# Four row tiles of the first three units multiplied into six open PSUM banks before the last four feature tiles are modulated

## The chip, the cores and the metric

The kernel runs on one core of one Trainium2 chip. The metric is device time in microseconds (us) of one launch; lower is better. A core has engines that run beside each other, each through its own list of instructions in order: TensorE (PE, matrix products into PSUM), VectorE (DVE), ScalarE (ACT), GpSimd (POOL) and SyncE (SP, which here only issues the transfers of weights). They wait for each other by semaphores. An engine whose next instruction waits does nothing else, and everything behind that instruction waits with it.

## The reference

A backbone of two layers on 512 tokens (256 of context, 256 latent) with 1024 features, all in float32. Each layer mixes tokens in three branches, and then has a feed-forward part. What this case touches is the very beginning of the first layer:

```python
mod_l = (jax.nn.silu(c) @ w_mod[l] + b_mod[l])[:, None, :]
sh1, sc1, g1, sh2, sc2, g2 = jnp.split(mod_l, 6, axis=-1)
# mixer_sublayer(x * (1.0 + sc1) + sh1, ..., w_in[l], ...), the context tokens with a modulation of their own:
(hq_l, hff_l, hfb_l, hi_l, hg_l, aq_l, ak_l, av_l, mz_l, mx_l, mdt_l, gt_l) = jnp.split(h_lat @ w_in, IN_SPLITS, axis=-1)
# branch C, mamba_inputs(mx_l, mdt_l, ...) and then ssd_scan:
u = jax.nn.silu(dwconv_centred(xbc, conv_w) + conv_b)
xs, bm, cm = jnp.split(u, [MB_INNER, MB_INNER + MB_BC_WIDTH], axis=-1)
dt = jax.nn.softplus(dt_raw.reshape(n, t, 2, MB_HEADS).astype(F32) + dt_bias.astype(F32))
```

Before the first product of `w_in` can run, the modulation's matrix must have been read as far as shift and scale go (2048 columns by 1024 rows of float32, 8 MB), and the tokens must have been scaled and shifted by it.

## The kernel before

**Products.** Every float32 operand is split into two float32r parts whose sum it is: `hh` and `hl` of the activations (eight row tiles of 128 features by 512 tokens), `wh` and `wl` of the weights. A product is then three matmuls, hi·hi, hi·lo, lo·hi (`mm3`, L347). A unit is 256 columns of a weight matrix: two output tiles of 128 columns, each in a PSUM bank of its own, summed over eight row tiles. That is 2 × 8 × 3 = 48 matmuls of 128x512 (`unit_f`, L360). PSUM has three banks for units (`pg`), four for all that is smaller (`ps`), and one more.

**Weights.** The class `Weights` streams all blocks through SBUF in one planned order. A block is 512 KB: four row tiles by 256 columns, so a unit has two, its first half (row tiles 0 to 3) and its second (4 to 7). SP issues a block's transfer (L115) into one of four buffers `wraw` (L150). When PE's program comes to a block, four further blocks have been asked for and two more split (L157): ACT copies the upper part `wh` (L125), DVE subtracts and leaves `wl` (L126); there are three buffers of each. A transfer into a buffer waits until the block that lay there four blocks earlier has been read, and SP's transfers go out in their order, so one that waits holds all behind it.

**Modulation.** 512 columns of the modulation come from four blocks of 256 rows (`mod_step`, L276). These blocks are not split: PE reads them from `wraw` itself, with 8 small matmuls a block, each recorded twice by the profile. After the fourth, DVE copies, transposes and adds the bias (L287 to L289). Columns j=0 and j=1 are the shift of feature tiles 0 to 3 and 4 to 7; j=2 and j=3 the scale of them. The modulation that is needed later comes as one block after every unit (`tick`).

**The start.** `run` (L1426) computes the modulation of j=0 and 2, loads feature tiles 0 to 3 of the tokens (on ACT's queue), and modulates and splits them (`modulate_first`, L322: two `h` instructions, `hh` on ACT, `hl` on DVE for a tile); the same for j=1 and 3 and feature tiles 4 to 7. `plan` (L1386) has the 16 blocks of this in the order j = 0, 2, 1, 3. `layer` (L1441) then calls `ssd_dt` (L619: a product of 64 columns, then a long chain of small DVE and ACT instructions `dx`, `dm`, `dy`, `dr`, `dz`, `dp`, at whose end PE transposes the result, `dtT`) and `ssd_in` (L714: units mx 0, mx 1 and bc of the first group; six tiles `craw` leave PSUM, each goes through a convolution of one ACT and four DVE instructions, L701). Then `Weave` (L72) lays the next group's units beside the first group's scan, which takes the convolved tokens (`xtok`), dt and, by a round trip to DRAM, the decays.

**Order.** A scheduler with a cost model of its own fixes each engine's order when the program is built; on the chip that order isn't changed.

Of the kernel before, what the change touches and what calls it, by code (L numbers as in the profile page):

```python
# [13 lines left out]
P = 128  # L14
DM = 1024
ND = 8
# [4 lines left out]
T = SEQ + CTX  # L21
ALPHA = (2 * DEPTH) ** 0.25
FFN = 2816
# [10 lines left out]
# columns of the per-channel parameters of a layer  # L34
# [19 lines left out]
def stagger(a, b, n):  # L54
    """a, and from its step n on b beside it"""
    for _ in range(n):
        next(a, None)
        yield
    live = [a, b]
    while live:  # L60
        for g in list(live):
            if next(g, g) is g:
                live.remove(g)
            else:
                yield
# [6 lines left out]
class Weave:  # L72
    """Two strands of work: the steps of the side strand are spread over those of the main one and stay a
    little behind it, so that the main strand's next products never queue behind the end of a side chain."""
# [4 lines left out]
    def __call__(self, main, side, nm, ns, lead=0, lag=0):  # L79
        """nm and ns: the steps of each, lag: the part of the side strand, in steps of main, left for the next call"""  # L80
# [11 lines left out]
class Weights:  # L92
    """Streams weight blocks [128, k, c] through SBUF: each block is loaded once
    and split into two float32r parts whose sum is the float32 value."""
# [49 lines left out]
class Net:  # L144
    def __init__(self, tc, io, ctx):
# [13 lines left out]
        self.weave = Weave()  # L159
        self.ticks, self.tick_plan, self.tick_run = [], 0, 0  # L160

# [4 lines left out]
    def x(self, name="x"):  # L166
        """like a, for tiles that would otherwise queue behind the other strand's"""
        return self.wp.tile([P, 512], F32, tag="x", name=name, bufs=self.n_x)
# [45 lines left out]
    def rsqrt(self, x, n):  # L214
        """x <- x ** -1/2 on a few columns: a first guess from the exponent and three Newton steps"""
# [46 lines left out]
    def lower_bounds(self):  # L262
        """the second layer's: the softmax over two layers as a sigmoid"""
# [7 lines left out]
    def mod_spec(self, l, j, c):  # L271
        """512 columns from 512 j, rows [256 c, 256 c + 256)"""
# [27 lines left out]
    def tick(self):  # L300
        """a piece of the modulations that are needed later"""
# [10 lines left out]
    def load_x(self, d0, d1):  # L312
        """feature-major tokens, [context | latent]"""
# [8 lines left out]
    def modulate_first(self, d0, d1):  # L322
        """h = x (1 + sc) + sh"""
# [23 lines left out]
    def mm3(self, out, xh, xl, yh, yl, first, last):  # L347
        """out += (xh + xl)^T (yh + yl)"""
# [4 lines left out]
    def plan_w(self, key, w, cols, kt=ND):  # L353
        """a unit: 256 columns of a weight matrix, in blocks of four row tiles"""
# [5 lines left out]
    def unit_f(self, key, rng, x=None, kt=ND):  # L360
        """feature-major: two tiles of 128 columns by the tokens rng[m]"""
        xh, xl = x or (self.hh, self.hl)
        out = [self.pg() for _ in rng]
        for h in range(0, kt, 4):
# [5 lines left out]
        self.tick()  # L370
        return out

    def unit_raw(self, key, ln):
        """two tiles of 128 columns before the layer norm's statistics are there: products with the rows times
        the gains, and with the gains and biases as two more tokens"""
# [20 lines left out]
    def raw_end(self, ln, e, j):  # L396
        """the statistics put in: a tile but for the bias, and the bias"""
# [7 lines left out]
    def raw_split(self, ln):  # L405
        """the next rows times the gains as split operands, with the gains and biases behind them"""
# [17 lines left out]
    def unit_t(self, key, js):  # L424
        """token-major: pairs js of token tiles by 256 columns"""
# [23 lines left out]
    def hgrn_in(self, l, p, wc, st):  # L449
        """projections of a pair of heads and everything that reads them from PSUM"""  # L450
# [38 lines left out]
    def hgrn_head(self, l, st, m, wc, oh, ol):  # L489
        """One head: attention over all pairs of tokens by levels of halving. At level h a block of 2h tokens  # L490
        is halved; the forward direction reads keys of the first half from queries of the second, the
        backward direction the other way. K = [forward | backward] keys times the decay to the end
        (start) of their half, Q = [backward | forward] queries times the decay over their half."""
# [10 lines left out]
        def total(h):  # L504
            """products of the decays over blocks of h, [forward | backward] of T / h each"""
# [5 lines left out]
        def grow(h):  # L511
            """to halves of 2h"""
# [106 lines left out]
    def ssd_dt(self, l):  # L619
        """step sizes, their logarithms and the decays' running sums, (stream, direction, head) on partitions"""  # L620
# [60 lines left out]

    def ssd_plan_x(self, l, g):
        w = self.io["w_in"][l]
        if g == 0 and l == 0:
            self.ssd_dt_plan(l)
        for i in range(2):
# [14 lines left out]
    def conv(self, l, r, n, t0):  # L701
        """depthwise conv over time, feature-major"""
# [11 lines left out]
    def ssd_in(self, l, g, wc, st, early=None):  # L714
# [13 lines left out]
        else:  # L728
            for i in range(2):
                ps = self.unit_f(("mx", l, g, i), [(0, T)] * 2)  # L730
                st["x"] += [self.conv(l, self.evac(ps[m], 0), 4 * g + 2 * i + m, 0) for m in range(2)]
                yield
            ps = self.unit_f(("bc", l, g), [(0, T), (q0, T)])
# [6 lines left out]
    def silus(self, tiles):  # L740
        """together, after the exponentials before them: one switch of the activation table"""
# [15 lines left out]
    def ssd_scan(self, l, g, st, dts, wc, ys):  # L757
        """both directions' scans of a group: within each stream by its decay matrix, from the context by its end states"""
# [85 lines left out]
    def ssd_out(self, l, g, ys, zs, wc, om):  # L844
        """gate and grouped RMS norm"""
# [23 lines left out]
    def quarters(self, tiles, n):  # L869
        """sum over partitions of every fourth tile, on 32 partitions each"""  # L870
# [9 lines left out]
    def colmean(self, tiles, n):  # L880
        """mean over partitions and tiles, on every partition"""
# [691 lines left out]
```

## Time and profile before

| | |
|---|---|
| three runs | 2701.3 to 2703.74 us, median 2702.61 |
| profiled execution: span | 2706.7 us |
| PE busy | 2619.4 us, 97% of the span |
| DVE busy | 1782.5 us, 66% |
| ACT busy | 1232.1 us, 46% |
| first two slices of 20 us: PE busy | 8.65 and 13.46 us |
| first two slices of 20 us: DMA engines' busy share | 0.91 and 0.98 |

For the profiled execution there is no time beside its span. It is 4.1 us over the median. PE is the busiest engine by far, yet in the first 40 us it has work for 22 us only, and the DMA engines are full: there the weights of the modulation arrive.

### The profile page before, as it was taken

The page shows a single profiled execution, that of the slowest core. Times are in us where ns is not written, and L with a number is a line of the kernel's source. Part 1 is how long each engine was busy: PE and PEld are TensorE (multiplying, and loading weights), DVE is VectorE, ACT ScalarE, POOL GpSimd, SP SyncE. Part 2 cuts the span into 40 slices and gives each one's busy share as a digit, 9 for nine tenths or more (in the row PEclk, how much of TensorE's full clock was granted, in tenths as well). Part 3 has the DMA queues.
Part 4 walks back from the last instruction along what each step waited for, and adds up shares of the span by engine and source line. Part 5 has one row for each costly group of instructions (what it writes and reads, how often), then busy time and mean ns, then how long its engine had stood idle before and what let it go on. Part 6 is the DMA issues. An engine that isn't in the chain of part 4 may idle for free.

```text
span 2706.7 us, 46300 instructions
## 1 busy us (share of the span) xinstructions
PE 2619.4 (97%) x18660; PEld 2148.0 (79%) x18660; DVE 1782.5 (66%) x3708; ACT 1232.1 (46%) x2030; POOL 192.4 (7%) x320
## 2 busy tenths in 40 slices
PE   7999999999999999999999999899999999999999
PEld 5767767788888897777888877677878898878998
DVE  5887776756555675456433367887867778867555
ACT  3555554532333324535432236566554344465543
POOL 0111010000000001100000000111110011111000
PEclk9999999999999999999999999899999999999999
DMA  6566555543444445352333323555763353445553
GB/s 238 152 179 176 150 164 149 155 123 114 122 135 130 128 125 172 105 175 63 101 94 101 94 78 90 140 164 154 212 183 108 97 144 109 144 131 181 169 182 102
DMA packets 298951, 374.41 MB, mean 138 GB/s; under 512 B 16432, under 2 KB 251984, under 8 KB 298736
## 3 DMA queue, kind: packets, MB, share of 16 engines
q1 hardware_dynamic: 271568, 284.21, 34.9%
q0 software_dynamic: 25728, 84.61, 11.0%
q8 instruction: 147, 2.41, 0.4%
q10 hardware_dynamic: 1440, 2.62, 0.3%
q14 instruction: 68, 0.56, 0.1%
HBM read 355.27 MB, written 16.12 MB: 137 GB/s over the span
## 4 chain that ended last, share of the span: by engine, by line
PE 69%; DVE 6%; DMA 3%; ACT 3%; issue 1%; POOL 0%; DVEq 0%; ACTq 0%; SPq 0%
PE g L204 56%; PE y L204 1%; PE PV L204 1%; PE S L204 1%; DVE wl L126 1%; DMA wraw<-in_w_in 1%; DMA ce<-sd 1%; PE o L204 1%; PE small L204 1%; PE cross L204 1%; PE mod L204 1%; PE PT L208 1%; PE lsq L204 1%; DVE s L196 1%; ACT wh L125 1%
## 5 line engine op out<-in xcount | busy, mean ns | idle before, releaser
L126 DVE TENSOR_TENSOR wl<-wraw,wh 128x1024 fp32r<-128x1024 f32 (+1 forms) x450 | 544.5, 1212 | 430.2 <-ACT wh L125 419.3
L125 ACT ACTIVATE wh<-wraw 128x1024 fp32r<-128x1024 f32 (+1 forms) x450 | 470.9, 1048 | 712.0 <-PE g L204 513.1
L204 PE MATMUL g<-hh,wh 128*128 128x512 f32 (+2 forms) x2032 | 733.5, 363 | 5.4 <-ACT wh L125 2.1
L204 PE MATMUL g<-hh,wl 128*128 128x512 f32 (+2 forms) x2032 | 726.2, 358 | 4.4 <-DVE wl L126 4.4
L204 PE MATMUL g<-hl,wh 128*128 128x512 f32 (+2 forms) x2032 | 725.9, 358 | 0.0
L204 PEld LDWEIGHTS g<-hh,wh 128*128 128x128 f32 (+1 forms) x2032 | 387.9, 191 | 77.4 <-issue 16.0
L204 PEld LDWEIGHTS g<-hh,wl 128*128 128x128 f32 (+1 forms) x2032 | 388.4, 191 | 66.4 <-issue 9.1
L204 PEld LDWEIGHTS g<-hl,wh 128*128 128x128 f32 (+1 forms) x2032 | 388.6, 191 | 61.8 <-issue 12.1
L204 PE MATMUL g<-oh,wh 128*128 128x512 f32 (+1 forms) x864 | 301.3, 350 | 2.6 <-DVE gl L193 1.5
L204 PE MATMUL g<-ol,wh 128*128 128x512 f32 (+1 forms) x864 | 295.6, 343 | 0.2 <-DVE ol L196 0.2
L204 PE MATMUL g<-oh,wl 128*128 128x512 f32 (+1 forms) x864 | 293.1, 340 | 0.5 <-DVE wl L126 0.5
L204 PE MATMUL g<-wh,hh 128*128 128x256 f32 x768 | 221.4, 288 | 0.0
L204 PE MATMUL g<-wh,hl 128*128 128x256 f32 x768 | 220.0, 286 | 0.0
L204 PE MATMUL g<-wl,hh 128*128 128x256 f32 x768 | 218.7, 285 | 0.0
L204 PEld LDWEIGHTS g<-oh,wh 128*128 128x128 f32 x864 | 163.9, 190 | 30.0 <-issue 8.1
L204 PEld LDWEIGHTS g<-ol,wh 128*128 128x128 f32 x864 | 164.3, 190 | 23.4 <-issue 7.1
L204 PEld LDWEIGHTS g<-oh,wl 128*128 128x128 f32 x864 | 163.9, 190 | 21.0 <-issue 3.6
L204 PEld LDWEIGHTS g<-wh,hh 128*128 128x128 f32 x768 | 147.6, 192 | 3.1 <-issue 2.6
L204 PEld LDWEIGHTS g<-wh,hl 128*128 128x128 f32 x768 | 147.7, 192 | 2.2 <-issue 1.9
L204 PEld LDWEIGHTS g<-wl,hh 128*128 128x128 f32 x768 | 147.6, 192 | 0.5 <-issue 0.4
L196 DVE SCALAR_TENSOR_TENSOR u<-craw,vec,u 128x508 f32<-128x508 f32 (+3 forms) x192 | 131.0, 723 | 10.0 <-ACT u L190 8.9
L196 DVE SCALAR_TENSOR_TENSOR D<-ab,tk,neg 128x128 f32<-128x128 f32 x384 | 110.3, 347 | 21.5 <-DMA ab<-sd 21.5
(303 smaller groups left out, 3600.3 us busy)
## 6 DMA issues: line engine op xcount, KB each, us to landing
wraw<-in_w_in SPq DMA_DIRECT2D x216, 512.0 KB, 4.1
wraw<-in_w_mod SPq DMA_DIRECT2D x96, 512.0 KB, 4.1
wraw<-in_w_ffn_in SPq DMA_DIRECT2D x88, 512.0 KB, 3.6
ab<-sd POOLq DMA_DIRECT2D x64, 512.0 KB, 6.9
wraw<-in_w_ffn_out SPq DMA_DIRECT2D x40, 512.0 KB, 3.4
ce<-sd POOLq DMA_DIRECT2D x64, 256.0 KB, 7.6
wraw<-in_w_br_mb SPq DMA_DIRECT2D x32, 512.0 KB, 3.4
wraw<-in_w_in SPq DMA_DIRECT2D x34, 256.0 KB, 3.5
```

The source lines that it names most:

```text
L125: self.nc.scalar.activation(hi[:, 0:n], t[:, 0:n], AF.Copy)
L126: self.nc.vector.tensor_tensor(out=lo[:, 0:n], in0=t[:, 0:n], in1=hi[:, 0:n], op=ALU.subtract)
L196: return self.nc.vector.scalar_tensor_tensor(out=out, in0=a, scalar=s, in1=b, op0=op0, op1=op1)
L204: return self.nc.tensor.matmul(out, l, r, start=start, stop=stop)
L208: return self.nc.tensor.transpose(out, in_, self.ident[0:k, 0:k])
```

## The change

The planned order of the weight blocks becomes: eight blocks of modulation (j=0 and 2), the first halves of the three units mx 0, mx 1 and bc, eight blocks of modulation (j=1 and 3), the second halves of the three units with a tick between them, and then the weights of dt, which used to come ahead of the units. After the first four feature tiles are modulated, `first_begin` computes the 72 matmuls of row tiles 0 to 3 of the three units. Their six sums stay open in all three `pg` banks and three of the four `ps` banks until `unit_f` adds row tiles 4 to 7. `layer` calls `ssd_in` ahead of `ssd_dt` in the first layer. All comments are taken out as well; helpers stand one line further down.

```diff
+        self.begun = {}
...
-    def unit_f(self, key, rng, x=None, kt=ND):
-        """feature-major: two tiles of 128 columns by the tokens rng[m]"""
+    def unit_f(self, key, rng, x=None, kt=ND, half=None):
+
         xh, xl = x or (self.hh, self.hl)
-        out = [self.pg() for _ in rng]
-        for h in range(0, kt, 4):
+        out = self.begun.pop(key, None) or [self.pg() for _ in rng]
+        for h in range(0, kt, 4) if half is None else (half,):
             wh, wl = self.w.take((key, h))
...
-        self.tick()
+        if half != 0:
+            self.tick()
         return out
...
+    def first_units(self):
+        w = self.io["w_in"][0]
+        return [(("mx", 0, 0, 0), [w[:, O_MX:O_MX + 256]]), (("mx", 0, 0, 1), [w[:, O_MX + 256:O_MX + 512]]),
+                (("bc", 0, 0), [w[:, O_MB:O_MB + P], w[:, O_MC:O_MC + P]])]
+
+    def first_plan(self, h):
+
+        for key, ws in self.first_units():
+            self.w.add((key, h), [w[P * h:P * h + 512, :].rearrange("(k p) c -> p k c", p=P) for w in ws])
+            if h:
+                self.plan_tick()
+
+    def first_begin(self):
+
+        outs = [[self.pg(), self.pg()], [self.pg(), self.ps("first")], [self.ps("first"), self.ps("first")]]
+        for (key, _), out in zip(self.first_units(), outs):
+            self.begun[key] = out
+            self.begun[key] = self.unit_f(key, [(0, T)] * 2, half=0)
+
     def ssd_plan_x(self, l, g):
         w = self.io["w_in"][l]
         if g == 0 and l == 0:
+            self.first_plan(4)
             self.ssd_dt_plan(l)
+            return
...
-                ps = self.unit_f(("mx", l, g, i), [(0, T)] * 2)
+                ps = self.unit_f(("mx", l, g, i), [(0, T)] * 2, half=4 if l + g == 0 else None)
...
-            ps = self.unit_f(("bc", l, g), [(0, T), (q0, T)])
+            ps = self.unit_f(("bc", l, g), [(0, T), (q0, T)], half=4 if l + g == 0 else None)
...
-        for j in (0, 2, 1, 3):
-            for c in range(4):
-                self.mod_spec(0, j, c)
+        for i in range(2):
+            for j in (i, 2 + i):
+                for c in range(4):
+                    self.mod_spec(0, j, c)
+            if i == 0:
+                self.first_plan(0)
...
             self.modulate_first(4 * i, 4 * i + 4)
+            if i == 0:
+                self.first_begin()
...
+            run(self.ssd_in(l, 0, wc, st[0]))
             dts = self.ssd_dt(l)
-            run(self.ssd_in(l, 0, wc, st[0]))
```

SP's list of transfers, from its start. A row gives the line, what is loaded from where, the block's shape and, where a row stands for several, their number. `in_w_mod` is the modulation's matrix, `in_w_in` the projection's; 128x8x64 is the weights of dt, and bc's block is two transfers of 128x4x128. Before:

```order
L229 DMA s<-in_cc 128x16
L115 DMA wraw<-in_w_mod 128x2x512 x16
L115 DMA wraw<-in_w_in 128x8x64
L115 DMA wraw<-in_w_in 128x4x256 x2
L115 DMA wraw<-in_w_mod 128x2x512
L115 DMA wraw<-in_w_in 128x4x256 x2
```

And SP's list from its start in the changed kernel:

```order
L230 DMA s<-in_cc 128x16
L115 DMA wraw<-in_w_mod 128x2x512 x8
L115 DMA wraw<-in_w_in 128x4x256 x2
L115 DMA wraw<-in_w_in 128x4x128 x2
L115 DMA wraw<-in_w_mod 128x2x512 x8
L115 DMA wraw<-in_w_in 128x4x256
L115 DMA wraw<-in_w_mod 128x2x512
L115 DMA wraw<-in_w_in 128x4x256
L115 DMA wraw<-in_w_mod 128x2x512
L115 DMA wraw<-in_w_in 128x4x128 x2
L115 DMA wraw<-in_w_mod 128x2x512
L115 DMA wraw<-in_w_in 128x8x64
```

Three blocks of the projection stand between the two halves of the first sixteen modulation blocks, and dt's weights moved from ahead of the six halves to behind them.

On PE, the end of the products ahead and what follows them in the changed kernel (`first` and `g` are the open sums, `mod` the modulation's small matmuls, 64 of which stand for eight blocks):

```order
L205 MATMUL first<-hh,wl 128x512
L205 MATMUL first<-hh,wh 128x512
L205 MATMUL first<-hl,wh 128x512
L205 MATMUL first<-hh,wl 128x512
L205 MATMUL mod<-wraw,sc 32x128 x73
L205 MATMUL g<-hh,wh 128x512 x3
L205 MATMUL first<-hh,wh 128x512
L205 MATMUL mod<-wraw,sc 32x128 x4
L205 MATMUL g<-hl,wh 128x512
```

Ahead of this piece stand 64 matmuls of the modulation and the rest of the 72 products; before, all 128 of the modulation stood together at the start and the products of dt came next. So on PE too the second eight modulation blocks (64 of the 73 matmuls) came to stand behind the 72 products.

On DVE, the beginning of dt's chain (`dx`, `dm`), in the kernel before:

```order
L193 TENSOR_TENSOR hl<-h,hh 128x512
L201 TENSOR_SCALAR h<-xin,s,mod_95 128x256 x2
L193 TENSOR_TENSOR hl<-h,hh 128x512
L126 TENSOR_TENSOR wl<-wraw,wh 128x1024
L200 TENSOR_SCALAR dx<-g,vec_93 64x256 x2
L126 TENSOR_TENSOR wl<-wraw,wh 128x1024
L200 TENSOR_SCALAR dm<-dx 128x256
```

And the beginning of dt's chain on DVE in the changed kernel, with the end of the convolutions (`u`) ahead of it:

```order
L126 TENSOR_TENSOR wl<-wraw,wh 128x1024
L197 SCALAR_TENSOR_TENSOR u<-craw,vec_93,u 128x2x254 x3
L197 SCALAR_TENSOR_TENSOR u<-craw,vec_93,u 128x2x255 x4
L197 SCALAR_TENSOR_TENSOR u<-craw,vec_93,u 128x2x254 x2
L126 TENSOR_TENSOR wl<-wraw,wh 128x1024
L201 TENSOR_SCALAR dx<-g,vec_93 64x256 x2
L126 TENSOR_TENSOR wl<-wraw,wh 128x1024
L201 TENSOR_SCALAR dm<-dx 128x256
```

All 24 convolution instructions of the first group, and two weight splits among them, now stand between the last `hl` and `dx`; before, one weight split stood there.

## Rows read from the trace of the kernel before

**Rows 1.** Page, part 1: busy time, share of the span, instructions.
```profile
PE 2619.4 (97%) x18660; PEld 2148.0 (79%) x18660; DVE 1782.5 (66%) x3708; ACT 1232.1 (46%) x2030; POOL 192.4 (7%) x320
```
**Rows 2.** Windows: us, busy us (instructions) of PE, PEld, DVE, ACT, POOL; clock; DMA; GB/s.
```profile
0.00:20.00 20.00, 8.65 (x128) 4.82 (x128) 2.77 (x13) 4.78 (x7) 3.00 (x9) 1.00 0.91 330
20.00:40.00 20.00, 13.46 (x140) 7.28 (x141) 11.47 (x27) 5.89 (x8) 0.00 (x0) 1.00 0.98 327
...
76.00:80.00 4.00, 4.00 (x10) 3.14 (x10) 3.84 (x7) 2.20 (x3) 0.00 (x0) 0.50 0.91 206
...
73.00:130.00 57.00, 56.94 (x316) 43.05 (x317) 44.52 (x73) 33.70 (x52) 3.57 (x5) 0.94 0.58 164
130.00:175.00 45.00, 44.18 (x257) 31.54 (x256) 41.87 (x87) 23.77 (x43) 7.77 (x11) 1.00 0.70 194
```
**Rows 3.** Timeline of SP: start, duration, what, [idle before <- released by].
```profile
1.18 25.53 SPq L115 DMA_DIRECT2D wraw<-in_w_mod  x16
27.84 3.38 SPq L115 DMA_DIRECT2D wraw<-in_w_in  x3
```
**Rows 4.** Waits of SP's queue, 0 to 110 us: total, times, longest.
```profile
SPq L115 <- PE mod L204: 23.9, 19, 3.5
```
**Rows 5.** Timeline of PE, modulation blocks (x16 is one block).
```profile
5.23 1.08 PE L204 MATMUL mod<-wraw,sc 128*32 128x128 f32 x16 [5.23 <-DMA wraw<-in_w_mod]
...
18.16 1.08 PE L204 MATMUL mod<-wraw,sc 128*32 128x128 f32 x16 [1.07 <-DMA wraw<-in_w_mod]
20.87 2.20 PE L204 MATMUL mod<-wraw,sc 128*32 128x128 f32 x32 [1.62 <-DMA wraw<-in_w_mod]
23.86 1.08 PE L204 MATMUL mod<-wraw,sc 128*32 128x128 f32 x16 [0.79 <-DMA wraw<-in_w_mod]
...
32.99 1.08 PE L204 MATMUL mod<-wraw,sc 128*32 128x128 f32 x16 [2.20 <-DMA wraw<-in_w_mod]
```
**Rows 6.** Timeline of PE, products and the transposes of dt.
```profile
35.19 0.69 PE L204 MATMUL g<-hh,wh 128*64 128x512 f32 x1 [1.12 <-ACT wh L125]
...
40.24 0.39 PE L204 MATMUL g<-hh,wh 128*128 128x512 f32 x1
...
67.15 0.39 PE L204 MATMUL g<-hl,wh 128*128 128x512 f32 x1
...
70.09 0.39 PE L204 MATMUL g<-hh,wl 128*128 128x512 f32 x1
73.02 0.33 PE L208 MATMUL dtT<-ident,dy 128*128 128x128 f32 x1 [2.54 <-DVE dy L193]
73.28 1.12 PE L204 MATMUL mod<-wraw,sc 128*32 128x128 f32 x32
...
83.51 0.39 PE L204 MATMUL g<-hh,wl 128*128 128x512 f32 x1
```
**Rows 7.** Page, part 5: DVE and ACT groups: busy, mean ns, idle before.
```profile
L126 DVE TENSOR_TENSOR wl<-wraw,wh 128x1024 fp32r<-128x1024 f32 (+1 forms) x450 | 544.5, 1212 | 430.2 <-ACT wh L125 419.3
L125 ACT ACTIVATE wh<-wraw 128x1024 fp32r<-128x1024 f32 (+1 forms) x450 | 470.9, 1048 | 712.0 <-PE g L204 513.1
...
L196 DVE SCALAR_TENSOR_TENSOR u<-craw,vec,u 128x508 f32<-128x508 f32 (+3 forms) x192 | 131.0, 723 | 10.0 <-ACT u L190 8.9
```
**Rows 8.** Timeline of DVE, modulation of feature tiles and start of dt's chain.
```profile
20.39 0.74 DVE L201 TENSOR_SCALAR h<-xin,s,mod 128x256 f32<-128x256 f32 x2
...
22.44 0.73 DVE L201 TENSOR_SCALAR h<-xin,s,mod 128x256 f32<-128x256 f32 x2
...
45.63 0.69 DVE L193 TENSOR_TENSOR hl<-h,hh 128x512 fp32r<-128x512 f32 x1 [0.70 <-ACT hh L190]
...
50.09 0.96 DVE L200 TENSOR_SCALAR dx<-g,vec 64x256 f32<-64x256 f32 x2
```
**Rows 9.** Timeline of PE, transposed tokens and the scan's first product.
```profile
96.12 1.97 PE L208 MATMUL xtok<-ident,u 128*128 128x128 f32 x16
...
127.19 0.65 PE L204 MATMUL y<-M,xt 128*64 128x256 f32 x2
```

## The prediction

> **What bounds the kernel now.** I read the busy shares first: TensorE (PE) works 97% of the span [rows 1], so a gain is a hole in PE that gets filled, a loss a new hole. The windows say where the holes are: in the first 40 us PE is busy for 8.65 and 13.46 us of 20 each, while the DMA engines are at 0.91 and 0.98 [rows 2]. From 73 to 130 us PE has no hole to speak of (56.94 of 57). So the stage that the change touches is bound by transfers up to about 34 us and by PE behind that. The timeline shows it in detail: the sixteen modulation blocks arrive one by one, PE waits for each, and the last is read at 32.99 + 1.08 = 34.1 us [rows 5]. The first product runs at 35.19, and from there PE hardly waits until dt's transposes at 73.02, for which it waits 2.54 us [rows 6]. DVE is the second engine: from 130 to 175 us it is busy for 41.87 of 45 us [rows 2].
>
> At the start SP issues sixteen loads and only then, from 27.84, the projection's [rows 3]. The waits of its queue say what paces it: PE's reading of modulation blocks, 19 times [rows 4]. That is the rule of four buffers: a load waits for PE to have read the block four places earlier.
>
> **What the change gains at first sight.** 72 products are taken out of the PE-bound stage. 13 products go from 67.15 to 70.09, 0.226 each [rows 6], so 72 are 16.3 us. They are to lie in the time in which PE waits for modulation blocks.
>
> **What the new order does to the loads.** In the changed lists both SP and PE have blocks 1 to 8 (j=0, 2), then the three projection blocks 9 to 11, then 12 to 19 (j=1, 3), and on PE all 72 products stand between block 8 and block 12. Blocks 12 to 15 fit into the four buffers. Block 16 may only be loaded once PE has read block 12, so after the last of the 72 products; blocks 17 to 19, the second halves and dt's weights stand behind it in SP's queue. The transfers, which bound this stage, therefore stop and wait for PE. How long is worked out in three steps.
>
> *End of the products ahead.* Blocks 9 to 11 land where 9 to 11 landed before, at 20.9, about 22.0 and 23.9 [rows 5]. A split takes ACT 1.05 and DVE 1.21 us [rows 7]: the first two `wl` end at 23.2 and 24.4. In DVE's new order they stand ahead of the first `h`, which before began at 20.39 [rows 8]; now it begins at 24.4, `hh` of the first tile is there at 25.8. A feature tile takes 22.44 − 20.39 = 2.05 us [rows 8], and a third split stands between: the fourth `hl` is there at 33.2. 48 of the 72 products stand behind it: 33.2 + 48 × 0.226 = 44.1. From the other end: after 6.6 us without work (block 8 ends at 19.24) PE is slow at first. In the kernel before, the first twelve products after a wait take 40.24 − 35.19 = 5.05 us instead of 2.7 [rows 6], a spacing of about 0.43; a stretch at that spacing shows a granted clock of 0.50, the 1.2 GHz level (the window from 76 us, [rows 2]). That way 25.8 + 5.05 + 60 × 0.226 = 44.4. I take 44.5.
>
> *Second half of the modulation.* Block 12 takes PE 0.56 us (two blocks 1.12, [rows 6]), so SP issues block 16 at 45.1. The first load of all went out at 1.18 and was read at 5.23 [rows 3, 5], 4.0 us; the next follow by (23.86 − 20.87) / 2 = 1.5 us [rows 5]. The four arrive at 49.1, 50.6, 52.1, 53.6, and the last step ends at 54.5: 20.4 us later than before (34.1). By the Trainium skill ("DMA: Bandwidth & Descriptors", section "Anatomy of one DMA — SWDGE (gpsimd) path", 2.0 us plus bytes by 436 GB/s) 512 KB would be an estimated 3.2 us, and everything here 0.8 us earlier; the row has 4.0 and is of this queue.
>
> *Second half of the features.* The second halves' weights land at about 55, 58 and 61 (a tick's block between each two). Their splits stand ahead of or between the `h` of DVE: first `wl` at 55 + 2.3 = 57.3, then four tiles of 2.05 and two more splits of 1.21: the last `hl` is there at 67.9. Before, it was 45.63 + 0.69 = 46.3 [rows 8].
>
> **The sum, in three terms.** *(a) PE up to the end of the first three units and dt.* After `hl` of tile 7, of PE's remaining 72 products 37 stand behind it by its order: 67.9 + about 1.6 (the last pieces at 0.43) + 37 × 0.226 = 78; a tick 0.56 and dt's 24 products 5.4: 84.0. In the kernel before, dt's products and the same three units end at 83.51 + 0.3 with one tick more [rows 6]. So the 16.3 us are spent on the wait, and (a) is 0, with ±5.
>
> *(b) dt.* Before, one weight split stands between the last `hl` and `dx`; now all 24 convolution instructions of the first group do, at 0.723 [rows 7], with two splits and dt's own (0.69): 67.9 + 0.7 + 17.4 + 2.4 = 88.4, with the waits for the six evacuations about 91 for `dx` (before 50.09, [rows 8]). The next unit's second half needs a `wl` that stands behind the convolutions too: PE reaches it at 84.0 + 24 × 0.226 = 89.4 and waits 1.5. dt's chain from `dx` to its transposes took 73.02 − 50.09 = 22.9 us [rows 6, 8], so 113.9; PE comes there, 120 products and a tick later, at 113 to 117, so no wait or up to 1. A wait of that size before cost 2.3 us of slow products besides [rows 6]. (b) is 5, from 0 (covered) to 10 (both waits in full with their slow products).
>
> *(c) The scan.* Before, 168 products stand on PE between dt's transposes and the first `y`, 54.2 us (73.02 to 127.19, [rows 6, 9]), which cover the way to DRAM and the decay matrices; now 73 stand there. From `xtok` to `y` it took 127.19 − 96.12 = 31.1 us [rows 9], with the next unit's convolutions between; PE's new work between the two is about 56 products and three blocks, 16.4 us with its transposes. The wait is between 0 (the convolutions were all that made the way long) and 14.7 (the way is no shorter); I take the middle, 7, and 2.3 for slow products: 9. DVE can't make it up quickly: before, it had 12.5 us to spare from 73 to 130 and 3.1 from 130 to 175 [rows 2], and it is about 13 us behind at hl of tile 7, having stood idle from 33 to 56 us.
>
> Sum: 0 + 5 + 9 = 14 us on the profiled span. That span, 2706.7, is the profiled execution's own time and 4.1 over the median of the runs: 2720.7 as a profile, 2716.6 as a time. DVE's lag should cost some more at the second group's scan, whose DVE window is full; I put 1.4 for it (0 to 3.1, what the window from 130 us has to spare) and predict 2718.
>
> **Rivals.**
> *1. Faster: the loads run on.* If blocks 16 to 19 did not wait for the 72 products, the second modulation would end only 3 × 1.5 = 4.5 us later than before, and 16.3 − 4.5 = 11.8 us would be gained: 2691. For it: the DMA engines are the bound there, and PE's list has room. Against: the rule of four buffers, and SP waited for PE's modulation matmuls 19 times already [rows 4]. It would be decided by SP's idle time between 28 and 45 us: none under this rival. Chance 0.04.
> *2. About even: the lag is swallowed.* (a) alone holds, dt and the decays come while PE still has other products: 0 to 5 us, 2703 to 2708. For it: PE waited for dt only once and DVE has 15.6 us to spare between 73 and 175 us. Against: DVE is 13 us behind and the stretch in which PE was covered shrinks from 168 products to 73. 0.11.
> *3. Slower by about 28: the products ahead all run slow.* They come in pieces, as each `hl` appears: 25.8 + 72 × 0.43 = 56.8 for their end, 12 us later than I have it, and all else with it: 2718 + 12 = 2730. For it: the first twelve after a wait of only 1.12 us were slow. Against: those behind were not, and 48 of the 72 stand in one piece behind the fourth `hl`. 0.07. The Trainium skill ("TensorE: Matmul & The Clock Gate", section "HAM oscillation — how this bites in real kernels") speaks for this rival: TensorE falls back to the slow clock when the work between waits for data is short, and is kept warm by long stretches; to cut the first units' sums in two around a wait for data is the opposite. The rows agree as far as they go (twelve slow products after a wait).
> *4. Slower by more than 20 through the scan:* (c) in full, 14.7 + 2.3, and once more in part at the second group: 2718 + 8 to + 14. 0.13.
> That the products do not in fact move is no rival: PE's list shows them.
>
> **How the numbers follow.** The forecast (2710 to 2726) has 0.65. A change below 0.2%, 5.4 us, can't be told from none here. Faster takes rival 1: 0.04. Same takes rival 2 but for a part: 0.09. Slower is the rest, 0.87. The range: rival 2 holds at 2703 to 2708, rivals 3 and 4 at 2726 to 2732; with 2707 to 2731 rival 1, most of rival 2 and the far end of 4 are left out.
>
> **What would show it.** SP idle from some 28 to 45 us, with PE's modulation matmuls as releaser. PE: products ahead from about 26 to 44.5, then idle for some 4 us, last modulation block at about 54; the last `hl` of tile 7 at about 68; the end of dt's products at 84; `dx` at about 91, the transposes at 114 to 117; a wait of `y` or of the decays ahead of it of several us. Wrong would be the prediction if the last modulation block were read before 45 us (rival 1), if PE were done with dt's products by 76, or if DVE reached `dx` before 80.

## The result, and the profile after

| | before | after |
|---|---|---|
| median of 4 runs each | 2703.18 us (2701.3 to 2704.98) | 2720.42 us (2714.04 to 2725.57) |
| profiled span | 2706.7 us | 2723.8 us |

The change made the kernel slower: ratio 1.0066, 95% interval 1.0052 to 1.0081, some 17 us.

PE's busy time over the whole span is the same to 1.3 us [rows 1]; of the 17.1 us by which the span grew, 15.8 are time in which PE does nothing:

```profile
PE 2620.7 (96%) x18660; PEld 2147.8 (79%) x18660; DVE 1781.8 (65%) x3708; ACT 1232.1 (45%) x2030; POOL 192.4 (7%) x320
```

The windows of the changed kernel, with the columns of [rows 2]:

```profile
20.00:40.00 20.00, 13.91 (x53) 10.87 (x54) 9.29 (x18) 5.70 (x7) 0.00 (x0) 1.00 0.52 170
40.00:60.00 20.00, 11.29 (x165) 8.06 (x163) 2.79 (x8) 1.06 (x1) 0.00 (x0) 0.76 0.64 206
...
73.00:130.00 57.00, 54.20 (x285) 41.61 (x284) 51.99 (x87) 33.77 (x49) 4.44 (x7) 1.00 0.42 118
130.00:175.00 45.00, 41.84 (x217) 28.46 (x216) 33.70 (x70) 23.41 (x42) 6.38 (x9) 0.92 0.56 156
```

From 20 to 40 us the DMA engines, at 0.98 before, are now at 0.52; from 40 to 60 DVE works 2.79 us of 20. From 130 to 175 us PE has holes and a mean granted clock of 0.92 (before 1.00, [rows 2]), that is, stretches at 1.2 GHz. Why the transfers stopped stands in SP's list (timeline) and in its waits from 0 to 75 us:

```profile
13.19 5.15 SPq L115 DMA_DIRECT2D wraw<-in_w_in  x4
19.46 28.85 SPq L115 DMA_DIRECT2D wraw<-in_w_mod  x8
```

```profile
SPq L115 <- PE mod L205: 34.4, 16, 18.3
```

The second eight modulation blocks were issued over 28.85 us, with one wait of 18.3 us for a modulation matmul of PE; before, the longest was 3.5 [rows 4]. PE's own list shows which:

```profile
18.31 1.08 PE L205 MATMUL mod<-wraw,sc 128*32 128x128 f32 x16 [0.95 <-DMA wraw<-in_w_mod]
26.09 1.65 PE L205 MATMUL g<-hh,wh 128*128 128x512 f32 x3 [6.70 <-ACT hh L191]
...
44.59 1.95 PE L205 MATMUL mod<-wraw,sc 128*32 128x128 f32 x64
49.19 0.64 PE L205 MATMUL mod<-wraw,sc 128*32 128x128 f32 x16 [2.65 <-DMA wraw<-in_w_mod]
53.04 1.08 PE L205 MATMUL mod<-wraw,sc 128*32 128x128 f32 x16 [3.20 <-DMA wraw<-in_w_mod]
...
56.45 1.08 PE L205 MATMUL mod<-wraw,sc 128*32 128x128 f32 x16 [1.04 <-DMA wraw<-in_w_mod]
...
88.47 0.39 PE L205 MATMUL g<-hh,wl 128*64 128x512 f32 x1
...
120.08 0.33 PE L209 MATMUL dtT<-ident,dy 128*128 128x128 f32 x1 [2.63 <-DVE dy L194]
...
150.79 1.09 PE L205 MATMUL y<-M,xt 128*64 128x256 f32 x2 [3.16 <-DVE M L194]
...
186.30 3.22 PE L205 MATMUL y<-M,xt 128*64 128x256 f32 x13 [7.17 <-DVE M L194]
```

Products ahead from 26.09 to 44.59, four modulation blocks from the buffers, then four that PE waits for one by one; the last ends at 57.5 (before 34.1, [rows 5]). dt's products end at 88.8. The first `y` runs at 150.79 instead of 127.19 [rows 9]. DVE's list answers to [rows 8]:

```profile
24.65 0.73 DVE L202 TENSOR_SCALAR h<-xin,s,mod 128x256 f32<-128x256 f32 x2
...
32.53 0.69 DVE L194 TENSOR_TENSOR hl<-h,hh 128x512 fp32r<-128x512 f32 x1 [0.70 <-ACT hh L191]
46.61 0.29 DVE L288 COPY modc<-mod 128x128 f32<-128x128 f32 x1 [13.38 <-PE mod L205]
...
57.60 0.29 DVE L288 COPY modc<-mod 128x128 f32<-128x128 f32 x1 [10.15 <-PE mod L205]
...
71.78 0.69 DVE L194 TENSOR_TENSOR hl<-h,hh 128x512 fp32r<-128x512 f32 x1 [0.70 <-ACT hh L191]
...
94.82 0.96 DVE L201 TENSOR_SCALAR dx<-g,vec 64x256 f32<-64x256 f32 x2
...
138.05 0.75 DVE L197 SCALAR_TENSOR_TENSOR u<-craw,vec,u 128x508 f32<-128x508 f32 x1 [7.33 <-ACT u L191]
```

Two gaps of 13.38 and 10.15 us, both until PE came past modulation steps; before, one of 4.77 us stood in their place:

```profile
34.14 0.29 DVE L287 COPY modc<-mod 128x128 f32<-128x128 f32 x1 [4.77 <-PE mod L204]
```

The waits of PE from 130 to 300 us (engine, line, waited for: us, times, longest), before and after:

```profile
PE y L204 <- DVE M L193: 2.4, 2, 1.6
```

```profile
PE y L205 <- DVE M L194: 11.5, 4, 7.2
```

The loss lies in the first layer. The loads of the HGRN2 branch's weights are sixteen in a run (eight in each layer); the last two times of a row are the first and the last of them. Before and after:

```profile
L115 SPq DMA_DIRECT2D wraw<-in_w_br_hg x16: 367/368/368, 976.6 to 2341.6; - x16
```

```profile
L115 SPq DMA_DIRECT2D wraw<-in_w_br_hg x16: 367/368/368, 999.8 to 2358.5; - x16
```

23.2 us are lost by the first layer's load, 16.9 by the second layer's. Between the two stands the same code in all kernels here; in the fourteen profiles of this study that stretch takes 1354.3 to 1365.9 us, and the profile of before (1365.0) is near the upper end. A single profile's total is uncertain by that much; below, the lag at the first layer's load stands beside the time.

### The profile page after: what moved, and what is told of

The parts are those of the page before. It is cut to its first block, busy times and chain, and to the rows that moved or that the text cites. A ratio compares the mean times of both kernels' runs of the same rounds, so it can differ in the third digit from the quotient of the medians.

```text
span 2723.8 us, 46311 instructions
## 1 busy us (share of the span) xinstructions
PE 2620.7 (96%) x18660; PEld 2147.8 (79%) x18660; DVE 1781.8 (65%) x3708; ACT 1232.1 (45%) x2030; POOL 192.4 (7%) x320
## 3 DMA queue, kind: packets, MB, share of 16 engines
q0 software_dynamic: 25728, 84.61, 10.8%
## 4 chain that ended last, share of the span: by engine, by line
PE 76%; DVE 8%; DMA 7%; issue 4%; ACT 3%; POOL 0%; SPq 0%; DVEq 0%; POOLq 0%; ACTq 0%
PE g L205 61%; DMA ce<-sd 2%; DMA ab<-sd 2%; PE y L205 2%; PE mod L205 2%; DVE wl L126 2%; DVE u L197 1%; PE PV L205 1%; PE S L205 1%; DMA wraw<-in_w_in 1%; PE o L205 1%; PE small L205 1%; PE cross L205 1%; DMA wraw<-in_w_mod 1%; PE csum L205 1%
## 5 line engine op out<-in xcount | busy, mean ns | idle before, releaser
L205 PE MATMUL g<-hh,wh 128*128 128x512 f32 (+1 forms) x2008 | 723.3, 363 | 12.4 <-ACT hh L191 8.8
L205 PE MATMUL g<-hh,wl 128*128 128x512 f32 (+1 forms) x2008 | 714.7, 357 | 4.5 <-DVE wl L126 4.5
L205 PE MATMUL g<-hl,wh 128*128 128x512 f32 (+1 forms) x2008 | 716.1, 357 | 0.0
L205 PEld LDWEIGHTS g<-hh,wh 128*128 128x128 f32 x2008 | 382.7, 191 | 86.4 <-issue 16.4
L205 PEld LDWEIGHTS g<-hh,wl 128*128 128x128 f32 x2008 | 383.4, 191 | 64.1 <-issue 7.0
L205 PEld LDWEIGHTS g<-hl,wh 128*128 128x128 f32 x2008 | 383.8, 191 | 60.6 <-issue 10.9
```

The costliest lines, as they stand in the source:

```text
L205: return self.nc.tensor.matmul(out, l, r, start=start, stop=stop)
```

## The experiments

Each was timed in five rounds beside the kernel before on the same chip. "Lag" is the time of the first of those loads less 976.6; for the last three columns of the kernel before see [rows 8] and [rows 9].

| kernel | median, over before | ratio (95%) | lag | last `hl` ends | `dx` | first `y` |
|---|---|---|---|---|---|---|
| the change | +17.2 | 1.0066 (1.0052 to 1.0081) | 23.2 | 72.5 | 94.8 | 150.8 |
| c_dt_last | +12.1 | 1.0052 (1.0039 to 1.0064) | 11.1 | 51.2 | 82.4 | 137.9 |
| e_between | +12.1 | 1.0051 (1.0038 to 1.0064) | 8.0 | 58.9 | 81.3 | 137.0 |
| a_two | +10.6 | 1.0045 (1.0032 to 1.0059) | 12.2 | 67.0 | 91.5 | 137.3 |
| b_two_dt_first | +8.7 | 1.0040 (1.0027 to 1.0052) | 3.7 | 66.2 | 68.2 | 137.9 |
| d_own2 | +7.9 | 1.0026 (1.0016 to 1.0036) | 4.4 | 61.8 | 86.8 | 134.8 |
| f_own2_dt_first | -1.6 | 0.9986 (0.9975 to 0.9997) | -6.3 | 52.8 | 53.5 | 123.2 |
| f_between_own2 | -3.7 | 0.9989 (0.9980 to 0.9998) | -5.8 | 54.8 | 55.6 | 127.0 |
| h_dt_conv | +21.9 | 1.0086 (1.0070 to 1.0101) | 21.6 | 71.4 | 87.7 | 151.7 |
| i_own_dt_conv | +15.7 | 1.0063 (1.0045 to 1.0080) | 13.3 | 62.0 | 80.3 | 144.7 |
| j_pool | +24.3 | 1.0101 (1.0086 to 1.0116) | 20.6 | 71.1 | 97.3 | 149.3 |
| k_own_pool | +11.0 | 1.0048 (1.0033 to 1.0063) | 12.5 | 55.1 | 55.9 | 130.7 |
| l_two_taps | +8.7 | 1.0035 (1.0020 to 1.0051) | 10.3 | 71.5 | 88.2 | 141.0 |

**c_dt_last: one part alone.** The kernel before with dt moved:

```diff
+            run(self.ssd_in(l, 0, wc, st[0]))
             dts = self.ssd_dt(l)
-            run(self.ssd_in(l, 0, wc, st[0]))
```

> The kernel before with one part of the change alone: dt's weights and products behind the first three units (no products ahead, the sixteen modulation blocks in one piece as before). Theory 1 (the loads held behind the 72 products cost most, because the second half of the features comes 20 us late; dt's place adds to it): the last hl stays at about 46 us, dx goes from 50 to about 80 (PE done with units and dt at about 76, convolutions as they come) instead of 94.8 in the changed kernel, the first group's scan loses a part of the 20 us that it lost there: 3 to 10 us slower than before. Theory 2 (dt's place is the whole loss, the late second half costs nothing by itself): 15 to 20 us slower than before, as the changed kernel.

Between the two theories, and above the first one's range: 12 us for the move of dt alone, with the second half of the features nearly in time (the last `hl` 4.9 us later than before).

```profile
82.40 0.97 DVE L200 TENSOR_SCALAR dx<-g,vec 64x256 f32<-64x256 f32 x2 [0.36 <-PE g L204]
```

`dx` starts 32 us later than before [rows 8], and the first `y` 10.7 us later.

**e_between: the loads less held, dt last.**

```diff
+        for k in range(4):
+            for (wh, wl), out in zip(ws, outs):
+                for m in range(2):
+                    if n % 2 == 0 and n // 2 < len(mods):
+                        self.mod_step(0, *mods[n // 2])
...
+                    self.mm3(out[m], a, b, self.hh[k], self.hl[k], k == 0, False)
```

> The changed kernel, but PE's eight modulation steps of j=1 and 3 stand between the products ahead, one after every six of them, instead of behind all 72; dt still last. Theory 1: SP is no longer held, the last modulation block is read at about 39 us instead of 57.5, the last hl is there at about 52 instead of 72, and of the changed kernel's 17 us over the time before 12 to 20 go away: 3 us faster to 5 slower than before. Theory 2 (dt's place): still 12 to 17 us slower than before.

The time is at the lower end of what the second theory had. The last modulation block ended at 45.7, not at 39, since each step still waits for six products; and the 12 us over before are what c_dt_last cost too, which fits a lead that is lost again at the scan with dt last. The next pair shows that dt's place is still not the whole.

**a_two and b_two_dt_first: fewer products ahead; and dt ahead of the second halves.** Two units ahead; in b, besides:

```diff
+            self.ssd_dt_plan(l)
             self.first_plan(4)
...
-            self.ssd_dt_plan(l)
...
+            dts = self.ssd_dt(l)
             run(self.ssd_in(l, 0, wc, st[0]))
-            dts = self.ssd_dt(l)
```

> The changed kernel with two units ahead instead of three: 48 products stand between the modulation halves, bc is computed whole behind them, dt last. Theory 1: the products ahead end at about 40 us instead of 44.5, all loads behind are 4 to 5 us earlier, and the time is 10 to 14 us over that of before instead of 17. Theory 2: unchanged, 15 to 19 over before.

> Two units ahead as in a_two, but dt's weights and products stand ahead of the second halves, so its chain starts before the convolutions. Theory 1: the second half is still 15 us late (last hl at about 67), dx at about 73 instead of 95 and its transposes at about 96; PE's loss up to there stays at about 5 us and the scan's shrinks: 4 to 9 us slower than before. Theory 2: no slower than before (-5 to +2 us).

a came out as the first theory had it. So did b: with dt ahead of the second halves the products ahead alone still cost 8.7 us. Two costs, then: dt's place (12 alone) and the products ahead (8.7 alone, for two units); together, in the change, 17. They overlap and do not add: a has both and costs 10.6, not 20. In time a and b, which differ in dt's place only, lie 1.9 us apart, less than the width of their intervals; by the lag of their profiles it is 8.5.

**d_own2, f_own2_dt_first, f_between_own2: the loads freed.** The second eight modulation blocks go to tiles of their own, which nothing else uses at the start:

```diff
+        if key in (("mod", 0, 1, 0), ..., ("mod", 0, 3, 3)):
+            t = [self.net.a(name="mraw") for _ in range(2)]
+            for k in range(2):
+                self._dma(t[k], parts[0][:, k, :])
...
```

> The changed kernel (three units ahead, dt last), but the eight blocks of j=1 and 3 are loaded into sixteen tiles of their own that are free at the start, in SP's order right behind the first halves, so that no load waits for PE to come past the 72 products. PE's order stays: it reads them behind the products. Theory 1 (the held loads are what the products ahead cost): the last modulation block is read at about 49 us instead of 57.5, the last hl is there at about 62 instead of 72, and 5 to 10 of the 17 us go away, down to what dt's place alone cost (12): 8 to 12 us slower than before. Theory 2 (the products ahead cost by their place on PE and by slow products, not by the loads): 15 to 18 slower, as the changed kernel.

> Two units ahead with dt ahead of the second halves (as b_two_dt_first, 8.7 us slower than before), and the second eight modulation blocks in tiles of their own. Theory 1: both causes are gone but for PE's order; the last modulation block is read at about 45 us instead of 50, the last hl at about 56 instead of 66, dx at about 60; 0 to 4 us slower than before. Theory 2: as b_two_dt_first, 7 to 10 slower.

> As f_own2_dt_first, and PE's modulation steps of j=1 and 3 stand between the 48 products, one after every three of them, instead of behind them. Theory 1: the last modulation block is read at about 40 us, the last hl at about 52, PE has no hole of more than 2 us from 26 us on and is about 5 us ahead of before by the end of the first three units; between 5 us faster and 1 slower than before. Theory 2 (splitting the sums costs by itself): 5 or more slower than before.

With three units and dt last, 9 of the 17 us go; with two units and dt first, all of them and a little more. Both are at or just beyond the fast end of their first theory's range (8 to 12 and 0 to 4 us slower). They differ in the number of units and in dt's place, so these two aren't told apart here. PE and DVE in f_own2_dt_first:

```profile
37.71 3.70 PE L224 MATMUL mod<-mraw,sc 128*32 128x128 f32 x128
...
52.06 0.69 DVE L213 TENSOR_TENSOR hl<-h,hh 128x512 fp32r<-128x512 f32 x1 [0.70 <-ACT hh L210]
53.53 0.97 DVE L220 TENSOR_SCALAR dx<-g,vec 64x256 f32<-64x256 f32 x2 [0.78 <-PE g L224]
```

All eight blocks lie ready when the products ahead end: 128 records without a gap. Against b_two_dt_first only the buffers differ (and SP's order, which sends these loads right behind the first halves), and the time falls by 10 us (last `hl` at 52.8 instead of 66.2). That shows the held loads as the cost of the products ahead. Both f kernels are faster than the kernel before by little (intervals to 0.9997 and 0.9998), and so faster than both kernels of this case. The interleaving of f_between_own2 brought nothing beyond, within their intervals.

**h_dt_conv and i_own_dt_conv: what holds the scan.** dt's chain ahead of the convolutions in the program, with loads held (h) and freed (i):

```diff
+            for key in [("mx", 0, 0, 0), ("mx", 0, 0, 1), ("bc", 0, 0)]:
+                raws += [self.evac(p, 0) for p in self.unit_f(key, [(0, T)] * 2, half=4)]
             dts = self.ssd_dt(l)
+            s0["x"] = [self.conv(l, raws[n], n, 0) for n in range(4)]
```

> The changed kernel, but with dt's chain ahead of the first group's convolutions in the program (PE's order of the first units and dt's products unchanged, loads held as in the changed kernel). If the scan's loss comes from dt's lateness: the loss up to dt's products stays (+5 us), dx comes at about 88 us instead of 95 and, no longer behind 24 convolutions, its transposes at about 107 instead of 120; the scan loses 5 to 12 us less than its 20: 6 to 12 us slower than before instead of 17. If it comes from the convolved tokens' lateness (the convolutions end later here): as slow as the changed kernel, 15 to 22 over before.

> Both at once for three units ahead: the second modulation's blocks in tiles of their own (d_own2, 8 us slower than before) and dt's chain ahead of the convolutions. If load holding and dt's lateness are the two causes and are independent: dx at about 77 us, transposes at about 97, no loss at the scan, -3 to +3 us against before. If the convolutions' lateness decides: as d_own2, 6 to 10 slower.

In both, what I had expected of dt's lateness fell. h_dt_conv came out as its other branch had it (15 to 22 us over before, measured 21.9), i_own_dt_conv as neither: it is 7.8 us slower than d_own2. In h_dt_conv (PE's and DVE's lists):

```profile
87.71 0.97 DVE L201 TENSOR_SCALAR dx<-g,vec 64x256 f32<-64x256 f32 x2 [4.11 <-PE g L205]
109.28 0.47 PE L209 MATMUL dtT<-ident,dy 128*128 128x128 f32 x1 [4.42 <-DVE dy L194]
119.66 0.70 DVE L197 SCALAR_TENSOR_TENSOR u<-craw,vec,u 128x508 f32<-128x508 f32 x1
151.74 0.65 PE L205 MATMUL y<-M,xt 128*64 128x256 f32 x2
```

dt's transposes come 10.8 us earlier than in the change, and `y` where it was. What was taken from dt's chain was put on the first group's convolutions, whose last (119.66) now ends at 120.4; in the change they ended before `dx`, at 93.8. So dt's chain by itself does not set the scan's start. The convolved tokens' lateness might, or that both must go through DVE. Three experiments went for the latter.

**j_pool and k_own_pool: part of DVE's work on GpSimd.**

```diff
-        self.nc.vector.tensor_tensor(out=lo[:, 0:n], in0=t[:, 0:n], in1=hi[:, 0:n], op=ALU.subtract)
+        eng = self.nc.gpsimd if 26 <= i < 56 and i % 2 else self.nc.vector
+        eng.tensor_tensor(out=lo[:, 0:n], in0=t[:, 0:n], in1=hi[:, 0:n], op=ALU.subtract)
```

> The changed kernel, with the subtraction of every second weight split between the 27th and the 56th block on GpSimd instead of DVE; five of them stand ahead of the first M (the decay matrices before the first y). If DVE is what sets the scan's start (in all kernels so far the first M comes at 20 us + 78 to 85 us of DVE work + DVE's idle time since 20 us): M comes 4 to 6 us earlier than 150.6, at about 145, and the time falls to 10 to 14 us over before, unless GpSimd's subtractions are so slow that PE waits for them. If dt's chain or the convolutions gate it by their latency alone: M stays at 149 to 152 and the time at 15 to 20 over before.

> The best so far (two units ahead, dt first, second modulation in tiles of its own: 1.6 us faster than before) with the same subtractions on GpSimd. If DVE sets the scan's start: M at about 117 instead of 122, but PE has no long hole there any more (1.6 us from 140 on), so little is left to gain: 1 to 6 us faster than before. If GpSimd's subtractions are slow: PE waits for wl, 0 to 6 us slower than before.

Both are slower than without the edit, and they decide nothing on the question, since DVE wasn't relieved (last section).

**l_two_taps: less work on DVE, nothing put elsewhere.** The kernel leaves out two of a convolution's five taps in the first two groups, so it computes something else and serves only to time the rest.

```diff
-        for j in (0, 1, 3, 4):
+        for j in (1, 3) if l == 0 and n in (0, 1, 2, 3, 4, 5, 6, 7, 16, 17, 20, 21) else (0, 1, 3, 4):
```

> The changed kernel with less work on DVE and nothing put elsewhere: in the first layer's first two groups each convolution leaves out its two outer taps, so two DVE instructions of 0.67 us a tile instead of four (24 fewer in all, nearly all of them ahead of the first M). The loads stay held. If DVE's throughput sets the scan's start: the last hl still at about 72 us and the last modulation block at about 57, but the first M 12 to 16 us earlier than 150.6, at 135 to 139, PE's loss behind 140 us shrinks from 20 to under 10, and the time is 0 to 9 us over that of before instead of 17. If what comes late comes late by the latency of the loads and of dt's chain alone: M at 145 to 151 and 13 to 19 us over before.

The windows from 20 us to the first M, of before, of the change, and of l_two_taps (the third pair of columns is DVE):

```profile
20.00:124.94 104.94, 95.82 (x554) 70.92 (x555) 77.33 (x140) 51.99 (x77) 4.69 (x8) 0.97 0.55 168
```

```profile
20.00:149.43 129.43, 108.04 (x641) 80.31 (x641) 83.94 (x153) 57.09 (x84) 5.16 (x8) 0.93 0.52 155
```

```profile
20.00:139.28 119.28, 101.05 (x593) 75.06 (x594) 67.09 (x123) 53.64 (x82) 5.17 (x8) 0.91 0.53 164
```

DVE has 16.9 us less to do, M comes 10.2 us earlier (I had put 12 to 16) and the time falls from 17.2 to 8.7 us over before, with the loads held nearly as long (last `hl` 71.5, not 72.5). DVE's list up to M thus holds the larger part of what sets the scan's start, not all: 6.7 us of the relief became idle time. Whether the relief worked through the convolved tokens or through what stands behind them on DVE, this kernel can't tell. Between before and the change DVE's work to the first M grew by 6.6 us (48 instead of 40 convolution instructions stand ahead of it), its idle time by 17.9 (27.6 to 45.5, the windows' lengths less DVE's busy time), of the 24.5 us that M is later. The two gaps of 13.38 and 10.15 us, in which DVE waits for the modulation that stands behind the held loads, are 18.8 us more than the 4.77 of before, so they make up this growth; the other gaps come to as much as before.

One of these others is a held load too, and stands on the way to M. DVE's wait of 7.33 us until 138.05 is for a convolution of the next group that ACT begins, and ACT first waits for a block of weights:

```profile
135.77 1.06 ACT L125 ACTIVATE wh<-wraw 128x1024 fp32r<-128x1024 f32 x1 [3.38 <-DMA wraw<-in_w_in]
```

SP issued this load at 127.68, right after a weight split of DVE from 126.43 to 127.65; from 75 to 140 us SP waited 42.8 us for such splits. The ring of four holds loads for DVE as it does for PE, and what is late on DVE comes back to DVE as late weights.

## Why the prediction was right

The time forecast, 2718, is 2.4 us from the median, and the mechanism was the one that the runs show: loads held behind the 72 products, and a way from dt to the scan that they no longer cover. That the number is so close is in part luck. Its terms were less exact than their sum: the first layer lost 23.2 us by the profiles where the terms make 15.4, and the second layer, which has no term, gave back 6.3.

*Loads held.* Right, to the step: the fourth `hl` ends at 33.2 (forecast 33.2), the products ahead at 44.6 (44.5), the first load behind them is read at 49.19 (49.1). The spacing of the other three was too small: read at 53.04, 54.33 and 56.45 instead of 50.6, 52.1 and 53.6. So the last block ended at 57.5, not 54.5, and the last `hl` at 72.5, not 67.9. The spacing had been taken from a stretch with full queues; here the transfers started from rest. That this is the reason isn't shown, and a part is this execution's own: in h_dt_conv, j_pool and l_two_taps, which begin as the change does, the last block ended at 55.2 to 55.4 and the last `hl` at 71.1 to 71.5.

*(a), forecast 0 with ±5:* dt's products end at 88.8 instead of 83.8: +5, at the edge of its bounds. Some 3 us come from that spacing, the rest mostly from DVE's waits for the second halves' weights between the `h` instructions, which the step had at nothing. The gain of 16.3 us was eaten, as the step had it.

*(b), forecast 5:* dt's transposes came at 120.08 (forecast 113.9), after a wait of 2.63 us. The like wait of 2.54 in the kernel before lies ahead of 83.8 [rows 6] and so is counted in (a). From the end of dt's products to the transposes PE stood idle for 2.8 us (31.38 us less 28.58 busy), with the granted clock at 1.00: (b) is about 3, since PE was late by nearly as much as dt and no slow products followed.

*(c) and its tail, forecast 9 and 1.4:* undersized. From dt's products (+5) to the first layer's load of the HGRN2 branch (+23.2) 18 us were lost, 3 of them in (b) and 15 here. From 130 to 300 us PE waited 11.5 us for M instead of 2.4, but only 3.16 of that for the first `y`; the longest wait, 7.17, is for a later M. Over the whole stretch (83.8 to 976.6 us before, 88.8 to 999.8 now) PE's idle time grew by 10.8 us and its busy time, for nearly the same work, by 7.4:

```profile
83.80:976.60 892.80, 876.53 (x7202) 694.39 (x7202) 612.58 (x1231) 395.67 (x626) 56.33 (x85) 1.00 0.50 143
```

```profile
88.80:999.80 911.00, 883.92 (x7190) 698.71 (x7189) 624.40 (x1263) 400.81 (x632) 59.35 (x90) 0.99 0.49 141
```

The longer busy time goes with the lower granted clock, 0.92 instead of 1.00 from 130 to 175 us. The step named too short a cover of PE's products over dt's way to the scan; what fills the way is mostly DVE's list, as l_two_taps showed and h_dt_conv suggests. That DVE "can't make it up quickly" stood there as a remark; it was the main thing.

*The second layer* wasn't in the sum. 6.3 us less were lost at the second layer's load, in code that is the same. How much of the first layer's 23 us is this profile's own chance, I can't settle.

*Rivals.* 1 (the loads run on, 2691) was excluded by SP's wait; that it needs more than free loads is shown by d_own2, which has them and is 7.9 us slower than before. 2 (lag swallowed): no, 18 us were lost behind dt's products. 3 (all 72 products slow): they took 44.59 − 26.09 = 18.5 us, 2.2 over the fast 16.3, so only the first ten or so were (26.09 to 30.40). The Trainium skill ("TensorE: Matmul & The Clock Gate", section "HAM oscillation — how this bites in real kernels") has in its example every short piece behind a wait start slow; the trace agrees for the start of this one, behind a wait of 6.70 us, and the 48 products at its end, with no wait ahead of them, ran at 0.226 us each. 4 (20 and more through the scan): behind dt's transposes 15 us were lost by the profiles, between the forecast's 10.4 and this rival's 18 to 24; without what the second layer gave back, the time would have been nearer to it.

## What to carry to other kernels

Before work is moved ahead into a wait for transfers, look at what the reader of those buffers does next: with a ring of four buffers, anything put between two readers on the reading engine holds the loads, and the wait is only moved. Give the loads that must run on buffers of their own first (here sixteen tiles that were free anyway), then fill the hole. And keep long chains of the second engine early, where it would idle: moving dt behind the convolutions cost 12 us by itself, though no engine had more to do in all. Moving the chain ahead on DVE alone, after PE had left its products to the end (h_dt_conv, i_own_dt_conv), didn't bring this back.

## What the runs showed of the hardware

GpSimd and DVE slowed each other. In j_pool two subtractions of 128x1024 on GpSimd took 9.19 us beside DVE's convolutions (timeline), 4.6 us each, and a later one 2.46 us; but beside that one a single convolution of DVE took 2.88 us:

```profile
83.00 9.19 POOL L127 TENSOR_TENSOR wl<-wraw,wh 128x1024 fp32r<-128x1024 f32 x2 [78.94 <-ACT wh L125]
106.34 2.46 POOL L127 TENSOR_TENSOR wl<-wraw,wh 128x1024 fp32r<-128x1024 f32 x1 [14.15 <-ACT wh L125]
106.47 2.88 DVE L198 SCALAR_TENSOR_TENSOR u<-craw,vec,u 128x508 f32<-128x508 f32 x1
```

And DVE's convolutions in the stretch from 83 to 92.2 us (groups: busy us, mean ns of one), in j_pool and in the change:

```profile
L198 DVE SCALAR_TENSOR_TENSOR u<-craw,vec,u 128x508 f32<-128x508 f32 (+1 forms) x7 | 9.1, 1357 | 0.0
```

```profile
L197 DVE SCALAR_TENSOR_TENSOR u<-craw,vec,u 128x510 f32<-128x510 f32 (+1 forms) x13 | 8.7, 744 | 0.0
```

1357 ns instead of 744, and 2.88 us where DVE's instruction began just behind GpSimd's and ended just behind it. The relief that moving a subtraction of 1.2 us was to give was lost in the neighbours' slower work: the time up to the first M held 86.2 us of DVE work with it and 85.2 without (from 20 us to the end of M). In k_own_pool it was 80.6 us up to the start of M, in f_own2_dt_first 76.8.
